# Start of a hybrid decoder step on one core: first loads and casts reordered, the norm's broadcast moved behind the second pair

## The chip, the cores and the metric

The kernel runs on one core of a Trainium2 chip. The metric is the device time of one launch in microseconds (us); lower is better. A core has TensorE (PE: matrix products), VectorE (DVE), ScalarE (ACT), GpSimd (POOL) and SyncE (SP, which here only issues loads and stores); all run beside each other and wait for each other through semaphores.

## What is computed

One step of a decoder block on T = 520 columns (512 prompt tokens and 8 sampled ones): a half-step SwiGLU FFN, a mixer with attention and state-space heads, a second half-step FFN, and a last norm. The change lies in the two FFNs, whose reference is:

```python
def rmsnorm(x, g):
    xf = x.astype(F32)
    y = xf * lax.rsqrt(jnp.mean(xf * xf, axis=-1, keepdims=True) + EPS) * g.astype(F32)
    return y.astype(x.dtype)

def half_ffn(x, norm_g, w_in, w_out):
    h = rmsnorm(x, norm_g)
    gate, up = jnp.split(h @ w_in, 2, axis=-1)
    return x + FFN_RESIDUAL * ((jax.nn.silu(gate) * up) @ w_out)
```

`D_MODEL` is 1024 and `D_FF` 2816, so `w_in` has 22 gate and 22 up tiles of 128 columns.

## The kernel before

**Layout.** x is held transposed, as 8 tiles `x[k]` of 128 x 520 (k runs over the 1024 rows of the model width). Each f32 value is kept as a rounded high part and a remainder: `cut` (lines 352 to 356) makes `qh` on ScalarE (line 354) and `ql` on VectorE (line 355) out of a weight tile of 128 x 512; `split_x` (lines 227 to 234) does the same for x times the norm's gain, giving `hh` (line 232) and `hl` (line 233). `mm3` (lines 212 to 224) then makes three matmuls for each product: high by high, high by remainder, remainder by high. A row of 520 columns is done in two halves f of 260, each in a bank of PSUM of its own.

**One FFN** is `ffn_comb` (lines 403 to 476); it is called twice, here named pass 1 (before the mixer) and pass 2 (after it). Its first loop runs over pairs j = 0 to 4 of a gate tile and an up tile. Pair 0 is done k by k for gate and up at once, pairs 1 to 4 first the gate (8 k's, 48 matmuls) and then the up. Pairs 0, 1 and 2 multiply x that is not yet normalised; their results are multiplied by the norm r afterwards. From pair 3 on, x itself has been normalised.

**The norm.** In pass 1 `first_squares` (lines 247 to 255) squares the eight tiles on ScalarE and adds them up in `acc` on VectorE. `rsq1` (lines 257 to 272) sums `acc` over the partitions on TensorE (line 263), takes the inverse root (line 265, a power on GpSimd, lines 283 to 286) and writes it to a diagonal `dg` (lines 269 and 271). `rsq_half2` (lines 496 to 505) spreads `dg` over all partitions with three matmuls (line 502) into the spare columns of the banks of pair 0, and ScalarE copies the result to `r` (line 504). `gate_up2` (lines 507 to 525) multiplies the banks of a pair by r (lines 516 and 517), which sets these banks free, and makes the hidden tile. `normalize` and `two` (lines 527 to 540) normalise x (line 531) and split it (`ch`, line 537, and `cl`, line 539).

**Banks.** PSUM has eight banks of this pool and a pair takes four. So pair 2 takes the banks of pair 0, and pair 3 those of pair 1.

**Order.** In `run`, the beginning stands under `manual_schedule` for SP, ScalarE and VectorE: these follow the order in which the code is written. In `ffn_comb` TensorE follows the written order, and the scheduler of the tile framework places the instructions of the other engines, among them the casts of later weight tiles, which may so come to stand in the middle of the manual part. Each load is counted on one of eight counters in turn (`DMAHW0` to `DMAHW7` in the lists below, SP and ScalarE together), and a load waits until the load before it on its counter has landed. Raw weights have names `fr` for pair 0 (`fr00`: gate, first half of the k's, `fr10`: up, `fr01`, `fr11`: second halves) and `br2`, `br3`, `br4` ... for the tiles after it: `br2` is the gate of pair 1, `br3` its up, `br4` the gate of pair 2. `setup_cache` loads five small tables (`pt`, `ci`, `v16`, `scv` on ScalarE's queue) and computes indices `ix` and `cwh` from them on VectorE.

Of the kernel before, what the change touches and what calls it, by code (L numbers as in the profile page):

```python
# [10 lines left out]
ALU = mybir.AluOpType  # L11
# [3 lines left out]
T = 520  # L15
NP = 512
HF = 260
D = 1024
# [126 lines left out]
class Program:  # L145
# [81 lines left out]
    def split_x(self, k, gcol):  # L227
        nc = self.nc
        hi = self.t2(f"hh{gcol}_{k}", F32R)
        lo = self.t2(f"hl{gcol}_{k}", F32R)  # L230
        g = self.vec[:, gcol + k:gcol + k + 1]
        nc.scalar.activation(hi[:, :T], self.x[k][:, :T], AF.Copy, scale=g)
        nc.vector.scalar_tensor_tensor(lo[:, :T], self.x[k][:, :T], g, hi[:, :T], ALU.mult, ALU.subtract)  # L233
        self.h[k] = (hi, lo)

# [167 lines left out]
    def ffn_comb(self, gcol, source, after=None, early=None):  # L403

        nc = self.nc
        self.b_more()
        with self.tc.manual_schedule(engines={mybir.EngineType.PE}):
            hid, held, r, norm = [], None, None, None
            for j in range(SFROM):
# [12 lines left out]
                for gu in range(len(pair), 2):  # L422
                    w = self.b_take()
                    ps = [self.bank1("gu") for _ in range(2)]
                    for k in range(8):
                        for f in range(2):
                            self.mm3(ps[f][:, :HF], w, k, self.h[k], f * HF, k == 0, k == 7)
                    pair.append(ps)
                    if held is not None:
                        r = self.rsq_half2(norm, held)  # L430
                        hid.append(self.gate_up2(*held, r))
                        held = None
                        h = self.normalize(r, gcol)
                    self.b_more()
                if r is None:
                    norm, held = self.rsq1(self.acc, D, pair[1][0][:, HF:], True), pair
                else:
                    hid.append(self.gate_up2(*pair, r if j < SRAW else None))
# [103 lines left out]
    def combos(self):  # L542
# [22 lines left out]
        for i, t in enumerate(tt):  # L565
            nc.vector.scalar_tensor_tensor(t[:, b], t[:, a], -1.0, self.xn[i + 4][:, a], ALU.mult, ALU.subtract)
# [157 lines left out]
    def setup_cache(self):  # L724
# [6 lines left out]
        for c0, c1, mul, col in ((0, 128, 128, 0), (128, 160, 32, 1), (160, 168, 8, 2)):  # L731
            nc.vector.tensor_scalar(ix[:, c0:c1], pt[:, c0:c1], mul, None, ALU.mult)
            nc.vector.tensor_tensor(ix[:, c0:c1], ix[:, c0:c1], ci[:, col:col + 1].to_broadcast([128, c1 - c0]), ALU.add)
# [7 lines left out]
        nc.vector.tensor_scalar_mul(self.cwh, self.vec[:, V_CW:V_CW + 40], 0.5)  # L741
# [781 lines left out]
    def run(self):  # L1523
        nc, tc, a = self.nc, self.tc, self.a
        with (
# [22 lines left out]
            with tc.manual_schedule(engines={mybir.EngineType.SP, mybir.EngineType.Activation, mybir.EngineType.DVE}):  # L1548
                warm = pc.tile([128, 1], F32, name="warm")
                nc.scalar.dma_start(self.vec, a["vec"])  # L1550
                nc.scalar.dma_start(self.x[0][:, :T], a["xT"][0])
# [3 lines left out]
                for c in range(2):  # L1555
                    for n in range(2):
                        nc.sync.dma_start(first[n][c], self.bu[n][1][:, c * 512:c * 512 + 512])
                    for k in range(4 if c else 1, 8 if c else 4):
                        nc.sync.dma_start(self.x[k][:, :T], a["xT"][k])
                self.b_load()  # L1560
                nc.sync.dma_start(self.cf, a["cf"])
                self.b_w = {n: ([], []) for n in range(2)}
                for k in range(8):
                    if k in (0, 4):
                        for n in range(2):
                            for q, t in zip(self.b_w[n], self.cut(first[n][k // 4])):
                                q.append(t)
                    self.split_x(k, V_F1)
                self.b_load()
                nc.sync.dma_start(self.cb, a["cb"])  # L1570
                self.b_load()
                self.first_squares()
                self.b_split()
# [48 lines left out]
```

## Time and profile before

| what | value |
| --- | --- |
| time, median of 3 runs | 1107.99 us (1107.32 to 1109.2) |
| the profiled execution's own time | 1109.26 us |
| its span, first to last instruction | 1107.5 us |
| PE busy | 1073.4 us, 97% |
| DVE, ACT, POOL busy | 719.4, 501.4, 264.6 us |
| PE on the chain that ended last | 86% |
| loads and stores | 204.30 MB, mean 184 GB/s |

TensorE is busy nearly all the time, so what counts is when it stands still, and at which clock it runs. The rows below show idle times with what ended them, and the granted clock behind some of them.

### The profile page before, as it was taken

To read this page: it belongs to the slowest core of one execution; us is meant where nothing else is said; L and a number is where in the kernel's file an instruction comes from. 1 tells how busy PE (TensorE), PEld (TensorE's weight loads), DVE (VectorE), ACT (ScalarE), POOL (GpSimd) and SP (SyncE) were. 2 spreads that over 40 slices of the span, in tenths; PEclk is the share of its full clock that TensorE was granted. 3 is DMA by queue.
4 is the path that set the end of the run, shared out by engine and by line. 5 is a ranking of instruction groups with operands and counts; after the bars stand their busy time and mean duration, and the time that the engine had idled before them with its cause. 6 is when DMAs were issued, how large, how long until landed. Compare 5 with 4: busy or idle time off the path is not lost.

```text
span 1107.5 us, 23255 instructions
## 1 busy us (share of the span) xinstructions
PE 1073.4 (97%) x9079; PEld 991.7 (90%) x9079; DVE 719.4 (65%) x1499; ACT 501.4 (45%) x1077; POOL 264.6 (24%) x261
## 2 busy tenths in 40 slices
PE   8999999999999999999999998999999999999995
PEld 6999999999999988776756676999999999999995
DVE  6985477467555679363768868449855764685563
ACT  6452355256244422456622555245534543562452
POOL 0001001110105667575343321120020011101013
PEclk9999999999999999999999999999999999999997
DMA  8539358455616788688899735163484584556302
GB/s 272 136 104 255 92 144 222 107 139 170 161 47 205 269 305 298 232 281 305 292 379 406 268 131 197 47 221 99 133 226 104 131 232 98 147 176 150 109 11 78
DMA packets 93917, 204.30 MB, mean 184 GB/s; under 512 B 13384, under 2 KB 21960, under 8 KB 89712
## 3 DMA queue, kind: packets, MB, share of 16 engines
q1 hardware_dynamic: 68736, 124.19, 34.4%
q0 software_dynamic: 22336, 77.08, 24.6%
q10 hardware_dynamic: 2736, 1.56, 0.5%
q8 instruction: 71, 1.16, 0.4%
q14 instruction: 38, 0.31, 0.1%
HBM read 191.78 MB, written 11.01 MB: 183 GB/s over the span
## 4 chain that ended last, share of the span: by engine, by line
PE 86%; DVE 5%; DMA 3%; issue 2%; ACT 2%; POOL 1%; ACTq 0%; DVEq 0%; SPq 0%; POOLq 0%
PE fo L223 7%; PE fo L224 7%; PE fo L222 7%; PE cx L578 6%; PE cx L577 6%; PE cx L576 6%; PE mps L222 4%; PE mps L223 3%; PE mps L224 3%; PE gu L222 3%; PE gu L224 3%; PE gu L223 3%; PE cy L576 3%; PE cy L577 3%; PE cy L578 3%; PE sps L1060 2%
## 5 line engine op out<-in xcount | busy, mean ns | idle before, releaser
L354 ACT CAST qh<-br 128x512 fp32r<-128x512 f32 (+1 forms) x310 | 168.2, 585 | 120.0 <-PE fo L223 57.5
L355 DVE TENSOR_TENSOR ql<-br,qh 128x512 fp32r<-128x512 f32 (+1 forms) x310 | 188.8, 644 | 44.1 <-ACT qh L354 19.3
L223 PE MATMUL fo<-hidl,qh 128*128 128x260 f32 x640 | 181.3, 283 | 0.8 <-DVE hidl L613 0.8
L222 PE MATMUL fo<-hidh,qh 128*128 128x260 f32 x640 | 181.1, 283 | 0.0
L224 PE MATMUL fo<-hidh,ql 128*128 128x260 f32 x640 | 180.8, 283 | 0.0
L578 PE MATMUL cx<-ch,ql 128*128 128x260 f32 x544 | 153.8, 283 | 0.0
L577 PE MATMUL cx<-cl,qh 128*128 128x260 f32 x544 | 153.6, 282 | 0.0
L576 PE MATMUL cx<-ch,qh 128*128 128x260 f32 x544 | 153.5, 282 | 0.0
L223 PEld LDWEIGHTS fo<-hidl,qh 128*128 128x128 f32 x640 | 120.4, 188 | 1.6 <-DVE hidl L613 1.5
L222 PEld LDWEIGHTS fo<-hidh,qh 128*128 128x128 f32 x640 | 120.5, 188 | 0.0
L224 PEld LDWEIGHTS fo<-hidh,ql 128*128 128x128 f32 x640 | 120.5, 188 | 0.0
L222 PE MATMUL mps<-hh,whi 128*128 128x260 f32 x384 | 113.3, 295 | 2.3 <-DVE raw L880 2.3
L348 POOL DMA_DIRECT2D br<-in_wi x34 | 29.7, 874 | 354.7 <-DMA br<-in_wi 204.7
L223 PE MATMUL mps<-hl,whi 128*128 128x260 f32 x384 | 109.7, 286 | 0.6 <-DVE hl L233 0.6
L224 PE MATMUL mps<-hh,wlo 128*128 128x260 f32 x384 | 109.4, 285 | 0.0
L576 PEld LDWEIGHTS cx<-ch,qh 128*128 128x128 f32 x544 | 102.4, 188 | 0.0
L578 PEld LDWEIGHTS cx<-ch,ql 128*128 128x128 f32 x544 | 102.4, 188 | 0.0
L577 PEld LDWEIGHTS cx<-cl,qh 128*128 128x128 f32 x544 | 102.3, 188 | 0.0
L786 POOL DMA_INDIRECT kv<-in_kc,ix x66 | 74.0, 1122 | 59.5 <-PE cy L578 25.7
L222 PEld LDWEIGHTS mps<-hh,whi 128*128 128x128 f32 x384 | 73.3, 191 | 13.5 <-issue 10.4
L577 PE MATMUL cy<-cl,qh 128*128 128x260 f32 x272 | 77.0, 283 | 0.0
L576 PE MATMUL cy<-ch,qh 128*128 128x260 f32 x272 | 76.9, 283 | 0.0
(430 smaller groups left out, 2705.4 us busy)
## 6 DMA issues: line engine op xcount, KB each, us to landing
br<-in_wi SPq DMA_DIRECT2D x206, 256.0 KB, 3.9
br<-in_wi POOLq DMA_DIRECT2D x68, 256.0 KB, 4.7
br<-in_wo SPq DMA_DIRECT2D x56, 256.0 KB, 2.9
wraw<-in_wm SPq DMA_DIRECT2D x24, 512.0 KB, 6.3
br<-in_wo SPq DMA_DIRECT2D x48, 128.0 KB, 2.7
kv<-in_kc SPq DMA_DIRECT2D x22, 256.0 KB, 4.6
spill<-xr SPq DMA_DIRECT2D x16, 260.0 KB, 3.3
xr<-spill SPq DMA_DIRECT2D x16, 260.0 KB, 5.5
```

The source lines that it names most:

```text
L222: mm(out, lhsT=hi[:, ks], rhs=xh[:, cs], start=start, stop=False)
L223: mm(out, lhsT=hi[:, ks], rhs=xl[:, cs], start=False, stop=False)
L224: mm(out, lhsT=lo[:, ks], rhs=xh[:, cs], start=False, stop=stop)
L348: nc.gpsimd.dma_start(s1, u[:, h[1]], accum_op=ALU.add)
L354: self.nc.scalar.copy(hi[:, :n], raw[:, :n])
L355: self.nc.vector.tensor_sub(lo[:, :n], raw[:, :n], hi[:, :n])
L576: mm(out, lhsT=hi[:, ks], rhs=xh, start=start and i == 0, stop=False, skip_group_check=True)
L577: mm(out, lhsT=hi[:, ks], rhs=xl, start=False, stop=False, skip_group_check=True)
L578: mm(out, lhsT=lo[:, ks], rhs=xh, start=False, stop=i == 3, skip_group_check=True)
L786: nc.gpsimd.indirect_dma_start(out=pages[j], out_offset=None, in_=a["kc"], in_offset=bass.IndirectOffsetOnAxis(ap=self.ix[:, 4 * n + j:4 * ...
L1060: nc.tensor.matmul(self.sbank[32 * hp:32 * hp + 32, cs], lhsT=self.qz[:, c0:c0 + 32], rhs=rhs(hp), start=(n % 16 == 0), stop=(n % 16 == 15 ...
```

## The change

It does four things. The first loads are all issued by SP in the order in which TensorE uses them, x[0] first, and the casts of the first weights are interleaved with the splits of x. The loads of pair 1 and of the gate of pair 2 are asked for right behind the split of x[3] (`issue_after`), and the cast of pair 1's gate is placed ahead of `first_squares`. The index computations of `setup_cache` are placed behind `self.mark`, the last of the combinations that are built for pair 5 on. And in `ffn_comb`, in both passes, the sum over the partitions (`rsq1`) moves from the end of pair 0 to before k = 6 of pair 1's gate, while the broadcast, the multiplications of pair 0 and `normalize` move from the end of pair 1's gate to the end of its up. The calls, tiles and matmuls stay the same in number.

```diff
--- before.py
+++ after.py
@@ -230,8 +230,8 @@
         lo = self.t2(f"hl{gcol}_{k}", F32R)
         g = self.vec[:, gcol + k:gcol + k + 1]
         nc.scalar.activation(hi[:, :T], self.x[k][:, :T], AF.Copy, scale=g)
-        nc.vector.scalar_tensor_tensor(lo[:, :T], self.x[k][:, :T], g, hi[:, :T], ALU.mult, ALU.subtract)
         self.h[k] = (hi, lo)
+        return nc.vector.scalar_tensor_tensor(lo[:, :T], self.x[k][:, :T], g, hi[:, :T], ALU.mult, ALU.subtract).ins
 
     def square_x(self, k, adder=None):
         nc = self.nc
@@ -423,17 +423,18 @@
                     w = self.b_take()
                     ps = [self.bank1("gu") for _ in range(2)]
                     for k in range(8):
+                        if j == 1 and k == 6 and gu == 0:
+                            norm = self.rsq1(self.acc, D, held[1][0][:, HF:], True)
                         for f in range(2):
                             self.mm3(ps[f][:, :HF], w, k, self.h[k], f * HF, k == 0, k == 7)
                     pair.append(ps)
-                    if held is not None:
+                    if j == 1 and gu == 1:
                         r = self.rsq_half2(norm, held)
                         hid.append(self.gate_up2(*held, r))
-                        held = None
                         h = self.normalize(r, gcol)
                     self.b_more()
                 if r is None:
-                    norm, held = self.rsq1(self.acc, D, pair[1][0][:, HF:], True), pair
+                    held = pair
                 else:
                     hid.append(self.gate_up2(*pair, r if j < SRAW else None))
                 if j == SRAW - 1:
@@ -563,7 +564,8 @@
             x0, x1 = self.xn[i], self.xn[i + 4]
             nc.vector.scalar_tensor_tensor(t[:, a], ss[i][:, b], -1.0, x0[:, a], ALU.mult, ALU.subtract)
         for i, t in enumerate(tt):
-            nc.vector.scalar_tensor_tensor(t[:, b], t[:, a], -1.0, self.xn[i + 4][:, a], ALU.mult, ALU.subtract)
+            self.mark = nc.vector.scalar_tensor_tensor(
+                t[:, b], t[:, a], -1.0, self.xn[i + 4][:, a], ALU.mult, ALU.subtract).ins
         halves(self.two(*tt), 6, 4)
 
     def product(self, out, w, p, start):
@@ -728,9 +730,10 @@
         nc.scalar.dma_start(pt, a["pt"])
         nc.scalar.dma_start(ci, a["ci"])
         ix = pc.tile([128, 168], I32, name="ix")
-        for c0, c1, mul, col in ((0, 128, 128, 0), (128, 160, 32, 1), (160, 168, 8, 2)):
-            nc.vector.tensor_scalar(ix[:, c0:c1], pt[:, c0:c1], mul, None, ALU.mult)
-            nc.vector.tensor_tensor(ix[:, c0:c1], ix[:, c0:c1], ci[:, col:col + 1].to_broadcast([128, c1 - c0]), ALU.add)
+        with self.tc.issue_after(self.mark):
+            for c0, c1, mul, col in ((0, 128, 128, 0), (128, 160, 32, 1), (160, 168, 8, 2)):
+                nc.vector.tensor_scalar(ix[:, c0:c1], pt[:, c0:c1], mul, None, ALU.mult)
+                nc.vector.tensor_tensor(ix[:, c0:c1], ix[:, c0:c1], ci[:, col:col + 1].to_broadcast([128, c1 - c0]), ALU.add)
         self.ix, self.ptr = ix, pt
         v16 = pc.tile([16, 3], F32, name="v16")
         nc.scalar.dma_start(v16, a["v16"])
@@ -738,7 +741,8 @@
         self.scv = pc.tile([128, 8, 4, 8], F32, name="scv")
         nc.scalar.dma_start(self.scv[:, :, 0:3, :], a["sc"].rearrange("p (c j b) -> p c j b", j=3, b=8))
         self.cwh = pc.tile([128, 40], F32, name="cwh")
-        nc.vector.tensor_scalar_mul(self.cwh, self.vec[:, V_CW:V_CW + 40], 0.5)
+        with self.tc.issue_after(self.mark):
+            nc.vector.tensor_scalar_mul(self.cwh, self.vec[:, V_CW:V_CW + 40], 0.5)
         self.kv_t, self.kv_pool = {}, {}
         self.ring = [n for n in range(64) if n not in KEARLY]
         self.sm = {}
@@ -1548,29 +1552,37 @@
             with tc.manual_schedule(engines={mybir.EngineType.SP, mybir.EngineType.Activation, mybir.EngineType.DVE}):
                 warm = pc.tile([128, 1], F32, name="warm")
                 nc.scalar.dma_start(self.vec, a["vec"])
-                nc.scalar.dma_start(self.x[0][:, :T], a["xT"][0])
+                nc.sync.dma_start(self.x[0][:, :T], a["xT"][0])
                 nc.scalar.activation(warm, self.mhalf, AF.Silu)
                 first = [[self.r2t(f"fr{n}{c}") for c in range(2)] for n in range(2)]
                 self.b_loaded = self.b_cut = 2
-                for c in range(2):
-                    for n in range(2):
-                        nc.sync.dma_start(first[n][c], self.bu[n][1][:, c * 512:c * 512 + 512])
-                    for k in range(4 if c else 1, 8 if c else 4):
-                        nc.sync.dma_start(self.x[k][:, :T], a["xT"][k])
-                self.b_load()
-                nc.sync.dma_start(self.cf, a["cf"])
+                def fetch(n, c):
+                    nc.sync.dma_start(first[n][c], self.bu[n][1][:, c * 512:c * 512 + 512])
+
+                fetch(0, 0)
+                for k in range(1, 8):
+                    if k in (1, 5):
+                        fetch(1, k // 4)
+                    if k == 4:
+                        fetch(0, 1)
+                    nc.sync.dma_start(self.x[k][:, :T], a["xT"][k])
                 self.b_w = {n: ([], []) for n in range(2)}
                 for k in range(8):
-                    if k in (0, 4):
-                        for n in range(2):
+                    for n in range(2):
+                        if k in (0, 4):
                             for q, t in zip(self.b_w[n], self.cut(first[n][k // 4])):
                                 q.append(t)
-                    self.split_x(k, V_F1)
-                self.b_load()
-                nc.sync.dma_start(self.cb, a["cb"])
-                self.b_load()
+                        if n == 0:
+                            mark = self.split_x(k, V_F1)
+                    if k == 3:
+                        with tc.issue_after(mark):
+                            self.b_load()
+                            nc.sync.dma_start(self.cf, a["cf"])
+                            self.b_load()
+                            nc.sync.dma_start(self.cb, a["cb"])
+                            self.b_load()
+                self.b_split()
                 self.first_squares()
-                self.b_split()
 
             def early():
                 self.leave("pg")
```

**ScalarE, start of pass 1**, from the split of x[5] on. Before:

```order
L232 ACTIVATE hh0_5_170<-x5_86,vec_76 128x520 [waits DMAHW6_49]
L232 ACTIVATE hh0_6_174<-x6_87,vec_76 128x520 [waits DMAHW7_49]
L354 CAST qh_328<-br3_182 128x512 [waits DMAHW4_49]
L232 ACTIVATE hh0_7_178<-x7_88,vec_76 128x520 [waits DMAHW0_49]
L252 ACTIVATE acc_191<-x0_81 128x520
```

Now:

```order
L232 ACTIVATE hh0_5_179<-x5_86,vec_76 128x520 [waits DMAHW6_49]
L354 CAST qh_328<-br3_158 128x512 [waits DMAHW4_49]
L232 ACTIVATE hh0_6_183<-x6_87,vec_76 128x520 [waits DMAHW7_49]
L232 ACTIVATE hh0_7_187<-x7_88,vec_76 128x520 [waits DMAHW0_49]
L354 CAST qh_191<-br2_153 128x512 [waits DMAHW1_49]
L354 CAST qh_195<-br2_155 128x512 [waits DMAHW2_49]
L252 ACTIVATE acc_199<-x0_81 128x520
```

The cast of the first half of `br3` stood behind the split of x[6] and now stands ahead of it; the casts of `br2` now come before the squares. The loads that these casts wait for stand now on SP like this, where counter 1 was last used by the load of `scv` on ScalarE's queue:

```order
L1568 DMA x6_87<-in_xT 128x520 [waits DMAHW7_49]
L1568 DMA x7_88<-in_xT 128x520 [waits DMAHW0_49]
L340 DMA br2_153<-in_wi1 128x512 [waits DMAHW1_49]
L340 DMA br2_155<-in_wi1 128x512 [waits DMAHW2_49]
L1580 DMA cf_77<-in_cf 128x530 [waits DMAHW3_49]
L340 DMA br3_158<-in_wi1 128x512 [waits DMAHW4_49]
```

**VectorE, pass 1**, from the last addition to `acc` to line 265. Before:

```order
L254 TENSOR_TENSOR acc_191<-acc_191,sq_211 128x520 [waits DVE_49,Activation_49]
L355 TENSOR_TENSOR ql_215<-br2_129,qh_214 128x512 [waits DMAHW1_49,Activation_49]
L355 TENSOR_TENSOR ql_219<-br2_131,qh_218 128x512 [waits DMAHW2_49,Activation_49]
L355 TENSOR_TENSOR ql_329<-br3_182,qh_328 128x512 [waits DMAHW4_49]
L265 TENSOR_SCALAR rsqt_340<-gu_230 128x5 [waits PE_49]
```

Now:

```order
L355 TENSOR_TENSOR ql_333<-br3_160,qh_332 128x512 [waits DMAHW5_49,Activation_49]
L254 TENSOR_TENSOR acc_199<-acc_199,sq_219 128x520 [waits DVE_49]
L355 TENSOR_TENSOR ql_409<-br4_163,qh_408 128x512 [waits DMAHW7_49,Activation_49]
L355 TENSOR_TENSOR ql_413<-br4_165,qh_412 128x512 [waits DMAHW0_49,Activation_49]
L355 TENSOR_TENSOR ql_530<-br5_336,qh_529 128x512 [waits DMAHW1_49,PE_49,Activation_49]
L355 TENSOR_TENSOR ql_534<-br5_338,qh_533 128x512 [waits DMAHW2_49,PE_49,Activation_49]
L355 TENSOR_TENSOR ql_604<-br6_416,qh_603 128x512 [waits DMAHW3_49,PE_49,Activation_49]
L355 TENSOR_TENSOR ql_608<-br6_418,qh_607 128x512 [waits DMAHW4_49,PE_49,Activation_49]
L265 TENSOR_SCALAR rsqt_378<-gu_230 128x5 [waits PE_49]
```

Between `acc` and line 265 three remainders of weights stood, and now there are six.

**TensorE, pass 1, end of pair 1.** The broadcast is followed by pair 1's up before, and now by pair 2's gate. Before:

```order
L502 MATMUL gu_229<-dg_352,cf_77 128x252 [waits DVE_49]
L502 MATMUL gu_231<-dg_352,cf_77 128x16 [waits DVE_49]
L222 MATMUL gu_479<-hh0_0_142,qh_328 128x260
```

Now:

```order
L503 MATMUL gu_229<-dg_390,cf_77 128x252 [waits DVE_49]
L503 MATMUL gu_231<-dg_390,cf_77 128x16 [waits DVE_49]
L222 MATMUL gu_553<-hh0_0_133,qh_408 128x260 [waits DVE_49]
```

What the new first matmul waits for on VectorE is the multiplication that sets the first bank of pair 0 free (line 517 of the changed kernel). The same holds in pass 2.

## Rows read from the trace of the kernel before

**Rows 1.** Windows, both stretches up to pair 3; columns: us, busy by engine, PEclk, DMA.

```profile
0.00:24.13 24.13, 18.74 (x108) 14.64 (x109) 14.37 (x29) 16.44 (x28) 0.19 (x4) 0.93 0.86 288
742.70:768.00 25.30, 25.30 (x211) 25.21 (x210) 21.70 (x46) 12.68 (x24) 3.07 (x3) 1.00 0.51 146
```

**Rows 2.** What PE waited for, first 35 us: us in total, times, longest.

```profile
PE gu L223 <- DVE hl L233: 2.1, 1, 2.1
...
PE gu L263 <- DVE acc L254: 0.7, 1, 0.7
```

**Rows 3.** Window with the granted TensorE clock (PEclk), start of pair 0.

```profile
10.38:13.36 2.98, 2.98 (x13) 2.98 (x14) 2.98 (x5) 2.37 (x4) 0.00 (x0) 0.50 1.04 367
```

**Rows 4.** Timeline of ACT and its queue, start: start us, us, what, idle before.

```profile
5.52 0.62 ACT L354 CAST qh<-fr 128x512 fp32r<-128x512 f32 x1 [0.57 <-DMA fr<-in_wi]
5.52 0.33 ACTq L729 DMA_DIRECT2D ci<-in_ci  x1
...
6.38 0.62 ACTq L739 DMA_DIRECT2D scv<-in_sc  x1
...
16.21 0.62 ACT L354 CAST qh<-br 128x512 fp32r<-128x512 f32 x1 [2.69 <-DMA br<-in_wi]
```

**Rows 5.** Timeline of SP's queue, the load of `br3` (both halves).

```profile
12.22 0.80 SPq L340 DMA_DIRECT2D br<-in_wi  x2
```

**Rows 6.** Weights `br` in the first 20 us: issue to landing.

```profile
DMA to landing us min/median/max: 4.0/5.6/5.7
```

**Rows 7.** Timeline of DVE, start to pair 1's first multiplication.

```profile
8.49 0.39 DVE L732 TENSOR_SCALAR ix<-pt 128x128 int32<-128x128 int32 x3 [1.63 <-DMA pt<-in_pt]
9.19 0.47 DVE L733 CUSTOM_DVE_ANT_0 ix<-ci,ix 128x256 uint16<-128x256 uint16 x3 [0.30 <-DMA ci<-in_ci]
...
13.46 2.09 DVE L233 SCALAR_TENSOR_TENSOR hl<-x,vec,hh 128x520 fp32r<-128x520 f32 x3
17.50 0.76 DVE L233 SCALAR_TENSOR_TENSOR hl<-x,vec,hh 128x520 fp32r<-128x520 f32 x1 [1.95 <-ACT hh L232]
18.55 5.52 DVE L254 TENSOR_TENSOR acc<-acc,sq 128x520 f32<-128x520 f32 x7 [0.29 <-ACT sq L252]
...
25.80 0.16 DVE L265 TENSOR_SCALAR rsqt<-gu 128x5 f32<-128x5 f32 x1
...
31.24 2.49 DVE L355 TENSOR_TENSOR ql<-br,qh 128x512 fp32r<-128x512 f32 x4
33.65 0.42 DVE L516 TENSOR_TENSOR gt<-gu,r 128x260 f32<-128x260 f32 x1
...
47.07 0.42 DVE L516 TENSOR_TENSOR gt<-gu,r 128x260 f32<-128x260 f32 x1
```

**Rows 8.** Timeline of PE, the first matmul of pair 3 in pass 1.

```profile
49.52 0.28 PE L222 MATMUL gu<-ch,qh 128*128 128x260 f32 x1
```

**Rows 9.** Timeline of PE in pass 2: broadcast, pair 1's up, pair 3.

```profile
749.60 1.14 PE L502 MATMUL gu<-dg,cf 128*128 128x252 f32 x6
750.60 0.37 PE L222 MATMUL gu<-hh,qh 128*128 128x260 f32 x1
...
767.95 0.28 PE L222 MATMUL gu<-ch,qh 128*128 128x260 f32 x1
```

**Rows 10.** Timeline of DVE in pass 2: first multiplications of pairs 0 and 1.

```profile
751.06 0.43 DVE L516 TENSOR_TENSOR gt<-gu,r 128x260 f32<-128x260 f32 x1
...
765.09 0.42 DVE L516 TENSOR_TENSOR gt<-gu,r 128x260 f32<-128x260 f32 x1
```

**Rows 11.** Timeline of PE in the mixer: two waits, in brackets.

```profile
439.49 0.36 PE L222 MATMUL mps<-hh,whi 128*128 128x260 f32 x1 [2.34 <-DVE raw L880]
...
577.56 1.10 PE L1251 MATMUL stp<-xdd,bn 128*128 128x256 f32 x4 [1.92 <-DVE xdd L1248]
```

**Rows 12.** Windows right behind these two waits.

```profile
439.40:443.00 3.60, 3.51 (x18) 3.54 (x19) 2.52 (x5) 1.01 (x3) 2.88 (x3) 0.60 0.77 209
577.50:582.00 4.50, 4.44 (x28) 2.17 (x28) 4.20 (x9) 0.59 (x1) 0.94 (x1) 1.00 1.00 390
```

## The prediction, before the changed kernel was run

> **What bounds the kernel now.** I read the busy times first, then the windows of the two stretches that the change touches, then what TensorE waited for in them, and last the timelines of the engines that it waited for. What to see: pass 1 has something to win and pass 2 has nothing. Up to 24.13 us TensorE is busy for 18.74 us and the clock is 0.93; in pass 2, from `rsq1` to pair 3, it is busy for 25.30 of 25.30 us at full clock [rows 1]. In pass 1 it waits 2.1 us for the remainder of x[0] and later 0.7 us for `acc` [rows 2], and behind the first wait it runs 2.98 us at the lower of its two levels, 1.2 instead of 2.4 GHz [rows 3]. One matmul of 260 columns costs 0.1205 us at the full clock: from 750.60 to 767.95 there are 48 of pair 1's up and 96 of pair 2 [rows 9], and 17.35 / 144 = 0.1205.
>
> **The start.** x[0] is loaded first and its split no longer stands behind the index computations, for whose tables VectorE waited until 8.49 and 9.19 [rows 7]. The second big load landed at 5.5 [rows 4]; `fr00` is second now, so ScalarE casts it at 5.5, splits x[0] at 6.1, VectorE makes the remainder from 6.8 to 7.55, and TensorE starts in earnest at 7.6. Without further waits it would need x[6] after 72 matmuls, at 7.6 + 8.7 = 16.3.
>
> The index computations now stand behind the last combination. What queues behind them is needed for pair 5, which is 192 matmuls or 23 us behind the start of pair 3; so they cost nothing here, and 0.9 us (0.39 + 0.47) if that cover were gone. SP's reads of the page table move too, to places where SP waits for a counter anyhow: nothing.
>
> **A new wait at x[6].** ScalarE is in order, and the cast of `br3` now stands ahead of the split of x[6]. When does `br3` land? `br2`, the first of the late loads, waits for counter 1, that is for `scv`. `scv` goes out once `fr00` has landed, at 5.55. Before, the load that waited for `scv` went out at 12.22, 5.84 us after `scv` at 6.38 [rows 4, 5]. So `br2` goes out at 11.4, not when x[3] is split; three issues of 0.4 us [rows 5] later, at 12.6, `br3`. It took 4.0 us before, issued at 12.22 and cast at 16.21 [rows 4, 5], so it lands at 16.6. The bounds: a load of `scv` as short as that of `ci`, 3.7 us (issued 5.52, used at 9.19 [rows 4, 7]), gives 14.45; a load of `br3` of 5.7 us, the longest [rows 6], gives 18.25. I take 16.6, since these are the same tiles in much the same queue. From that cast to the start of VectorE's split behind the next one were 1.29 us (16.21 to 17.50 [rows 4, 7]): x[6]'s remainder starts at 17.9.
>
> The Trainium skill, page "DMA: Bandwidth & Descriptors", section "Anatomy of one DMA — SWDGE (gpsimd) path", gives 2.0 us plus the bytes at 436 GB/s for one transfer on another issuing path. An estimate by that page puts `scv` at 2.2 and `br3` at 2.6 us, the cast at 11.6, and the end where rival C below has it. The trace disagrees, with 5.84 and 4.0 us.
>
> **VectorE from there to pair 3.** It has no gap of its own, so this is a sum [rows 7]: the remainders of x[6] and x[7] 2 x 0.67 (three take 2.09); three remainders of weights at 0.60 (31.24 to 33.65 is four), 1.8; six additions to `acc`, 5 x 0.80 + 0.6 (seven take 5.52, each waiting for the one before), 4.6; a remainder 0.6, the last addition 0.6; six remainders 3.6; from line 265 to the end of `dg` 5.44 before (25.80 to 31.24), less the one remainder that is no longer in between, 4.9; two remainders 1.2. Together 18.7, so pair 0 is multiplied from 36.6. TensorE agrees: `acc` is ready 9.0 us after 17.9, at 26.9; the sums take 1.0, then 12 + 48 matmuls 7.2, so the broadcast starts at 35.2; and in pass 2 the multiplication came 1.46 us behind the broadcast (749.60 to 751.06 [rows 9, 10]): 36.7. I take 36.7.
>
> Two new waits follow, because the banks are now set free late. Pair 2's gate needs the first bank of pair 0, free 0.42 us after 36.7, at 37.1. Pair 3 needs the first bank of pair 1, which VectorE reaches behind eight normalisations and eight remainders of x: 13.42 us after pair 0's first multiplication (33.65 to 47.07 [rows 7]), by the same 23 instructions as before, and 0.42 for itself: 50.55. TensorE would be there at 37.1 + 96 x 0.1205 = 48.7 and waits 1.85. Before, pair 3 started at 49.52 [rows 8]. **Pass 1: +1.0 us**, all that the early start won being given back; its bounds, from the landing of `br3`, are -1.1 and +2.7.
>
> **Pass 2** has only the losses. Count from the broadcast. Before, the next matmul came 1.0 us later (749.60 to 750.60 [rows 9]). Now it waits for the bank until 1.46 + 0.42 = 1.9: +0.9. Pair 3 can start at 1.9 + 11.57 = 13.45 by TensorE, but the bank of pair 1 is free at 1.46 + 14.03 (751.06 to 765.09 [rows 10], the same 24 instructions) + 0.42 = 15.9: +2.45. **Together +3.35 us.** Before, both lay beside pair 1's up, whose 48 matmuls are 5.8 us. The bounds are narrow, 0.3 us, since each length has its row.
>
> **The clock.** A wait of 2.34 us for VectorE was followed by a window at 0.60 mean granted clock, one of 1.92 us by a window at 1.00 [rows 11, 12]. The wait before pair 3 is 1.85 in pass 1 and 2.45 in pass 2, so I let the clock fall in pass 2 alone. The price: 0.40 x 3.60 = 1.4 us in that window; at the start 2.98 us at 0.50 are 1.5 [rows 12, 3]. **+1.5 us**, with 0 and 1.7 as its bounds. The Trainium skill, page "TensorE: Matmul & The Clock Gate", section "Loop structure matters more than you think", says that VectorE copying a result out of PSUM does not break TensorE's warmth. By that rule this term is nothing and the sum is rival B's. The row at 439.49 speaks against it, a wait for VectorE with a slow window behind it.
>
> **The sum**: 1.0 + 3.35 + 1.5 = +5.85 us. The profiled execution took 1109.26 us, its span 1107.5 and 1.76 around it; that is 1.27 over the median of 1107.99. So I expect 1115.1 for that one, and 1113.8 as the median. Behind pair 3 the order is nearly as before and TensorE works without a pause, so I carry the difference to the end.
>
> **Rivals.**
> - B: the clock holds. For it: 2.45 is hardly more than 2.34, and TensorE was busy throughout before it. Against: those two rows. +4.35, 1112.3.
> - C, not slower: the cast of `br3` costs nothing and the early start is kept. Place: ScalarE, ahead of x[6]; price: 1 us at pair 3 for each us that `br3` lands earlier, until TensorE itself is the bound: 7.6 + (96 + 36 + 60 + 96) x 0.1205 + 1.0 + 1.9 + the 1.85 is 47.05, 2.5 us earlier than before. With the clock holding, the total is +0.85, 1108.8. It decides from a landing at 14.4 on, where the total is 2.2. Against it: my lower bound is 14.45, and it needs the clock too. For it: a chain of estimated landings.
> - D: the clock falls in pass 1 also, behind the 1.85 us or the wait at x[6]. For it: 1.85 is close to 1.92, which has one row alone. +7.35, 1115.3.
>
> **Numbers.** The forecast 0.45, B 0.28, D 0.12, C 0.10, something else 0.05. A measurement of this kernel can tell about 0.2%, 2.2 us, from no change. Forecast, B and D are slower by more; C is within it; to be faster both passes would have to lose less than I can construct. That gives slower 0.85, same 0.12, faster 0.03. The range: at its low end the clock holds and pass 1 is at its lower bound, -1.1 + 3.35 = +2.25, 1110.2; at its high end 2.7 + 3.35 + 1.7 + 1.5 = +9.25, 1117.2. It leaves out C, and I round to 1110 and 1117.
>
> **What would show it.** In the new profile: TensorE in earnest at about 7.6; a ScalarE wait for `br` ahead of x[6], until about 16.6; pair 3 of pass 1 near 50.5 with a wait for line 517 of the changed kernel; in pass 2 two waits for the same line, 0.9 and 2.45 us; a lower granted clock behind the second. I am wrong if the two waits of pass 2 are missing (then the banks did not bind), or if ScalarE does not wait for `br3` (then pass 1 wins).

## The result: slower, by about the forecast amount, with two of its terms wrong in size

The changed kernel takes 1114.26 us (median, 1113.19 to 1116.67) against 1107.99. The medians lie 6.3 us apart; the recorded ratio is 1.0065, interval 1.0047 to 1.0083, which is +7.2 us with 5.2 to 9.2. Timed again later (`e11_changed_again`) the ratio was 1.0054 (1.0034 to 1.0074), and the medians lay 6.9 us apart. The gains and losses below go by the recorded ratios. The forecast was 1113.8 and a range of 1110 to 1117.

The page of the changed kernel, busy times and the chain that ended last; TensorE's share of the chain was 86% before and is 81% now, VectorE's was 5% and is 8%:

```profile
span 1114.0 us, 23258 instructions
...
PE 1076.7 (97%) x9079; PEld 993.6 (89%) x9079; DVE 720.1 (65%) x1499; ACT 501.4 (45%) x1077; POOL 263.9 (24%) x261
...
PE 81%; DVE 8%; DMA 4%; ACT 3%; issue 3%; POOL 1%; SPq 0%; DVEq 0%; ACTq 0%; POOLq 0%
```

What TensorE waited for in the changed kernel (us in total, times, longest), first from 0 to 60 us, the stretch of [rows 2], then from 735 to 800:

```profile
PE gu L222 <- ACT hh L232: 3.6, 2, 2.7
PE gu L222 <- DVE gt L517: 2.4, 2, 1.7
...
PE gu L223 <- DVE hl L234: 0.6, 2, 0.4
```

```profile
PE gu L222 <- DVE gt L517: 3.1, 2, 2.3
```

The 2.1 us for the first remainder and the 0.7 for `acc` are gone. In their place stand 2.7 us for the split of x[6], and in each pass two waits for line 517, the multiplication that sets a bank free. In pass 2 TensorE had not waited at all [rows 1].

Windows of the changed kernel: up to the end of the wait at x[6], behind it, around pair 3 of pass 1, and behind the wait before pair 3 of pass 2 (PEclk is the third number from the end):

```profile
0.00:18.87 18.87, 13.93 (x84) 10.38 (x84) 7.26 (x12) 8.96 (x14) 0.19 (x4) 1.00 0.88 279
18.87:25.70 6.83, 6.32 (x27) 6.02 (x28) 6.13 (x10) 6.83 (x14) 0.00 (x0) 0.50 0.97 359
51.80:56.00 4.20, 2.54 (x22) 2.54 (x22) 4.20 (x9) 1.04 (x2) 0.00 (x0) 1.00 0.01 4
...
773.20:776.63 3.43, 3.43 (x19) 3.43 (x18) 3.34 (x8) 1.27 (x2) 0.00 (x0) 0.50 0.00 0
```

The clock fell behind the wait at x[6] and behind the one in pass 2, and not behind the 1.66 us in between.

To see where the time went, each execution is cut at three matmuls, whose starts stand in TensorE's timelines (pair 3 of pass 1, the first of pass 2, pair 3 of pass 2), and at its end. The first column is a time, the other three are distances. The last four rows come from a slower chip, on which more below.

| kernel | pair 3, pass 1 | to the first of pass 2 | to its pair 3 | to the end |
| --- | --- | --- | --- | --- |
| before [rows 8, 9] | 49.52 | 681.73 | 36.70 | 339.55 |
| before, second profile (`e10`) | 49.61 | 679.11 | 36.70 | 339.63 |
| changed | 53.49 | 679.06 | 40.17 | 341.24 |
| changed, second profile (`e11`) | 50.91 | 681.82 | 40.17 | 341.20 |
| `e1` new start alone | 56.07 | 682.53 | 36.80 | 339.67 |
| `e2` norm's new place alone | 52.77 | 678.54 | 40.16 | 341.71 |
| `e3` br3 behind | 49.28 | 679.21 | 40.16 | 340.94 |
| `e4` pair 1 first | 50.30 | 679.74 | 37.83 | 340.41 |
| `e9` spread | 44.59 | 677.58 | 36.76 | 339.86 |
| `e5` before, slower chip | 49.66 | 724.56 | 36.70 | 339.50 |
| `e6` scv on another queue | 51.22 | 720.95 | 40.17 | 342.45 |
| `e7` squares first, old norm | 47.95 | 726.58 | 36.70 | 339.64 |
| `e8` squares first, new norm | 51.49 | 723.76 | 40.18 | 341.02 |

In the third column the norm's late place shows alike to 0.1 us wherever it stands as the change has it. Pass 1 is not alike: the two profiles of the changed kernel differ by 2.6 us. And the second column moves by 2.7 us between two profiles of one kernel, in either direction. It holds the rest of pass 1 as well; that rest, up to the last matmul of the pass's output product (`fo`), takes 323.6 to 324.1 us in all nine profiles that are not from the slower chip, so the movement is the mixer's, and the moved index computations cost no more than half a microsecond there. They were not tried alone.

### The profile page after: what moved, and what is told of

Read it like the earlier page. It is cut to its first block, busy times and chain, and to the rows that moved or that the text cites. A ratio compares the mean times of both kernels' runs of the same rounds, so it can differ in the third digit from the quotient of the medians.

```text
span 1114.0 us, 23258 instructions
## 1 busy us (share of the span) xinstructions
PE 1076.7 (97%) x9079; PEld 993.6 (89%) x9079; DVE 720.1 (65%) x1499; ACT 501.4 (45%) x1077; POOL 263.9 (24%) x261
## 4 chain that ended last, share of the span: by engine, by line
PE 81%; DVE 8%; DMA 4%; ACT 3%; issue 3%; POOL 1%; SPq 0%; DVEq 0%; ACTq 0%; POOLq 0%
PE fo L223 7%; PE fo L224 7%; PE fo L222 7%; PE cx L578 6%; PE cx L579 6%; PE cx L580 6%; PE mps L222 3%; PE mps L223 3%; PE mps L224 3%; PE cy L578 3%; PE cy L579 3%; PE cy L580 3%; PE sps L1064 3%; PE gu L222 2%; PE gu L223 2%
## 5 line engine op out<-in xcount | busy, mean ns | idle before, releaser
L222 PEld LDWEIGHTS mps<-hh,whi 128*128 128x128 f32 x384 | 72.4, 188 | 13.3 <-issue 10.2
```

The source lines that it names most:

```text
L222: mm(out, lhsT=hi[:, ks], rhs=xh[:, cs], start=start, stop=False)
```

## The experiments

### The two halves of the change, each alone

`e1_start_only` is the changed kernel with the loop over pairs put back:

```diff
-                        if j == 1 and k == 6 and gu == 0:
-                            norm = self.rsq1(self.acc, D, held[1][0][:, HF:], True)
...
-                    if j == 1 and gu == 1:
+                    if held is not None:
                         r = self.rsq_half2(norm, held)
                         hid.append(self.gate_up2(*held, r))
+                        held = None
                         h = self.normalize(r, gcol)
...
-                    held = pair
+                    norm, held = self.rsq1(self.acc, D, pair[1][0][:, HF:], True), pair
```

> Only the start's reordering is kept, the norm stands where it stood before. Theory M (the late cast of br3 stops the start, and the norm's late place stops both passes): the wait at x[6] stays (2.7 us, then half clock to about 25.7); acc is ready at 28.2 as in the changed kernel, and now TensorE stands about 3 us for it; pair 3 of pass 1 starts 25.4 us behind the first sum, at 53.6, +4.1 against before; pass 2 is as before, no wait for pair 0's or pair 1's banks, no fall of the clock. Total +1.3 to +4.1 (the mixer gave back 2.8 us in the changed kernel's profile), 1109.3 to 1112.1. Rival N (the norm's late place is the whole loss, the new start only wins): pair 3 at 47 to 48.5, total -1 to -2.5, 1105.5 to 1107.

Measured: ratio 1.0069 (1.005 to 1.0087), +7.6 us. What TensorE waited for up to 60 us, and a window that begins inside the longest wait:

```profile
PE gu L263 <- DVE acc L254: 5.3, 1, 5.3
PE gu L222 <- ACT hh L232: 3.0, 2, 2.0
```

```profile
24.67:34.91 10.24, 7.72 (x36) 7.72 (x37) 7.29 (x20) 3.57 (x8) 2.60 (x2) 0.50 0.41 122
```

Rival N falls: the new start costs as much by itself as the whole change. Theory M had the place right and the size wrong, pair 3 standing at 56.07 instead of 53.6: the wait for `acc` was 5.3 us instead of 3, since the clock held behind x[6] this time and TensorE was there at 21.9, while `acc` was ready at 27.13, only 1.1 us sooner than in the changed kernel. The clock was at half for 10.24 us, of which TensorE worked 7.72. Pass 2 is as before.

`e2_norm_only` is the reverse of this edit, made in the kernel before.

> Only the norm is moved, the start is the one of before. Theory M: the 0.7 us for acc goes; in pass 1 TensorE waits 0.9 us before pair 2 and 1.9 before pair 3, which starts at 51.3, +1.8; in pass 2 the same two waits, 0.8 and 2.3 us, +3.5, and behind the second the clock falls for 3.4 us, +1.5. Total +6.8, less up to 2.8 in the mixer: 1112.0 to 1114.8. Rival S (the start's order is the whole loss, the norm's place costs nothing): 1108, no wait for the multiplication by r ahead of pair 3.

Measured: 1.0065 (1.004 to 1.009), +7.2 us. In pass 2:

```profile
PE gu L222 <- DVE gt L517: 3.1, 2, 2.3
```

The same line as in the changed kernel. Rival S falls. Pass 1 lost 3.2 us instead of 1.8: the clock was at half from 7.6 to 14.4, and TensorE waited 0.7 us for a remainder. Each half costs about 7 us and both together cost 7, so the parts overlap in pass 1: with the new start `acc` comes late, and the later `rsq1` does not wait for it, which saves the 5.3 us of `e1`.

### br3 behind, and pair 1 first

`e3_br3_behind`, a second `b_split` in the written order, so that the scheduler can't place the casts of `br3` ahead of x[6]:

```diff
                 self.b_split()
+                self.b_split()
                 self.first_squares()
```

> The changed kernel with the casts of br3 behind those of br2, so behind the splits of x[6] and x[7]. Theory M: no wait at x[6], no half clock at the start; TensorE reaches the sums earlier, and pair 3 of pass 1 starts at about 48.1 instead of 53.5, where VectorE's chain lets it; pass 2 keeps its +3.5 and the clock's +1.5. Total -5.4 against the changed kernel, 1108.9; 1111.7 if what the mixer gave back there goes with it. Rival L (the loads of the second pair land too late for any order: TensorE stands for br2 or acc instead): pair 3 at 52 or later, 1113 to 1114.

Measured: 1.0049 (1.0033 to 1.0066), +5.4 us, pair 3 at 49.28. The wait at x[6] is gone and the clock holds to the end of pass 1, as theory M has it, but the gain is smaller. Up to 60 us:

```profile
PE gu L222 <- DVE gt L517: 2.5, 2, 1.7
PE gu L263 <- DVE acc L254: 2.1, 1, 2.1
```

The wait moved on to `acc`: ScalarE now waits for `br2` and `br3` ahead of the squares. Against the mean of the two profiles of the changed kernel (52.2) pass 1 won 2.9 us; I had counted from the later of the two. So rival L is half right: TensorE does stand for `acc`, and the median of 1113.06 us lies where L has it; pair 3, which L has at 52 or later, lies near theory M's 48.1.

`e4_pair1_first` multiplies pair 1 by r before x is normalised, and leaves it out where it stood:

```diff
                         r = self.rsq_half2(norm, held)
                         hid.append(self.gate_up2(*held, r))
+                        hid.append(self.gate_up2(*pair, r))
                         h = self.normalize(r, gcol)
...
-                else:
+                elif j > 1:
                     hid.append(self.gate_up2(*pair, r if j < SRAW else None))
```

> The changed kernel with pair 1 multiplied by r before x is normalised, in both passes, so that pair 1's banks come free early. Theory M: the wait before pair 3 of pass 2 goes from 2.3 to about 0.5 us (now for the first split tile), and with it the fall of the clock behind it: -1.8 - 1.5; in pass 1 from 1.66 to about 0.3. Total -4.6 against the changed kernel, 1109.6. Rival K (the clock's fall in pass 2 has another cause than this wait): the slow stretch at 773 stays, 1111.1. Rival V (VectorE is the bound whatever its order: pair 3 waits as long for its split tiles): 1114.

Measured: 1.0008 (0.9995 to 1.0022), +0.9 us, 5 to 6 less than the changed kernel. TensorE's waits from 735 to 800, and the window around pair 3 of pass 2:

```profile
PE gu L222 <- DVE gt L518: 0.8, 1, 0.8
PE gu L223 <- DVE cl L541: 0.6, 1, 0.6
```

```profile
766.00:775.00 9.00, 8.36 (x69) 8.15 (x69) 9.00 (x18) 4.42 (x9) 0.00 (x0) 1.00 0.11 29
```

The bank's 2.3 us are 0.6 for a split tile, and the clock stays at 1.00. From the first matmul of pass 2 to the end it is 378.24 us against 381.41, 3.2 less, where 3.3 were expected. In pass 1 the wait of 1.66 us is gone too. Rivals K and V fall: the order on VectorE was the bound, not its work, and the slow stretch comes with that wait. `e4` is one profile, but the other six without that wait have no such stretch either, and all six with it do.

### scv on another queue

Four runs (`e5` to `e8`) fell on a chip where the kernel before takes 1155.24 us; they are compared with each other. `e5_before_again` is the kernel before, unchanged.

> The kernel before, unchanged, profiled a second time. Theory M holds that the 2.8 us which the changed kernel seems to win in the mixer are the chance of one execution: the mixer of before shows other waits and other slow stretches of the clock this time, and from pair 3 of pass 1 to the broadcast of pass 2 it is 1 us or more shorter than in the first profile, while pair 3 of pass 1 stands at 49.5 within 1 us and pass 2 loses nothing. Rival P (the changed kernels really win in the mixer, because they come to it with another timing): the mixer is as long as in the first profile, within 0.5 us.

What differs there lies between about 350 and 565 us, in the end of pass 1 and in the mixer. TensorE stands idle for nothing that the profile shows, 19.4 us in all, and from pair 3 to pass 2 the granted clock is at half for 41.0 us, where it was 6.8 in the first profile of before. Two of the waits in `e5` (`fo` is the end of pass 1), and a window of it (PEclk third from the end):

```profile
PE sps L1060 <- issue: 6.2, 13, 1.0
...
PE fo L222 <- issue: 3.5, 6, 1.3
```

```profile
330.00:470.00 140.00, 120.86 (x953) 105.49 (x953) 79.72 (x152) 37.66 (x67) 69.04 (x65) 0.88 0.65 214
```

In the first profile of before the clock of the same window was 0.99. So `e5` says nothing on the mixer of the first chip, and cannot tell theory M from rival P; pair 3 (49.66) and pass 2 (36.70) are as there.

`e6_scv_other_queue`:

```diff
-        nc.scalar.dma_start(self.scv[:, :, 0:3, :], a["sc"].rearrange("p (c j b) -> p c j b", j=3, b=8))
+        nc.gpsimd.dma_start(self.scv[:, :, 0:3, :], a["sc"].rearrange("p (c j b) -> p c j b", j=3, b=8))
```

> The changed kernel with the load of scv on GpSimd's queue, so that no load of SP waits for it. Theory M (br2 went out at 11.14 because its counter waited for scv): br2 goes out at about 9.2, right behind the last x; br3 at about 11.6 (its counter then waits for x[4]) instead of 12.47, and is cast at 16.4 to 17.0 instead of 17.87; the wait at x[6] shrinks from 2.7 to 1.3 to 1.9 us. Rival Q (the queue or the memory is the limit, not the counter): br3 is cast at 17.5 or later and the wait stays at 2.4 or more.

The issues of the weights on SP's queue, and the cast of `br3`, in `e6`:

```profile
9.19 0.90 SPq L340 DMA_DIRECT2D br<-in_wi  x2
...
10.62 0.93 SPq L340 DMA_DIRECT2D br<-in_wi  x2
```

```profile
16.93 0.62 ACT L354 CAST qh<-br 128x512 fp32r<-128x512 f32 x1 [4.29 <-DMA br<-in_wi]
```

`br2` goes out at 9.19 as expected, so the counter and `scv` did hold it, and rival Q's times are not met. `br3` goes out at 10.62, a microsecond sooner than expected, and takes 6.3 us. The wait at x[6] was 1.4 us, inside theory M's span; but in `e11`, with `scv` where it was, the cast came at 16.32, and the changed kernel did not run on the chip of `e6`. What the counter is worth at x[6] is therefore not settled: how long the weights take to land moves as much.

### Squares ahead of the casts, with either place of the norm

`e7` puts the squares first and the norm where it stood; `e8` has the same start and the norm of the changed kernel.

```diff
-                self.b_split()
                 self.first_squares()
+                self.b_split()
+                self.b_split()
```

> The new start with the squares ahead of the casts of br2 and br3, and the norm where it stood before. Theory M: no wait at x[6], acc ready at about 18.6, the sums at 18.8 instead of 24.13 and pair 3 of pass 1 18.35 us behind a broadcast at 25.6 to 26.5, at 44.3 to 45.5, -4 to -5.2 against before; pass 2 as before. Total 1103 to 1104.5. Rival L (the second pair's loads are the limit of pass 1): TensorE waits for br2 or br3 instead, pair 3 at 47 or later, 1106 or more.

> As the run beside it, but with the norm's late place of the changed kernel. Theory M: the broadcast of pass 1 at 31.4, pair 3 15.3 us behind it, at 46.7, -2.8 against before, and pass 2 loses 3.5 and 1.5 for the clock: total +2.2, 1110.2; against the run beside it the norm's place costs 7 us, though nothing waits for acc in either. Rival N2 (the norm's late place costs only where something else is late too): within 2 us of the run beside it.

Measured: `e7` 0.9985 (0.9969 to 1.0001), pair 3 at 47.95; `e8` 1.0043 (1.0028 to 1.0058), pair 3 at 51.49. Between them 0.58%, 6.7 us (the medians: 6.2), where 7 were expected, and rival N2 falls: the late place costs this also with an early `acc`. Of it 4.9 are in pass 2 (40.18 + 341.02 against 36.70 + 339.64). But both miss their own times, and pair 3 of `e7` stands where rival L has it, at 47 or later. TensorE's waits up to 60 us in `e7`, then in `e8`:

```profile
PE gu L263 <- DVE acc L254: 2.1, 1, 2.1
```

```profile
PE gu L222 <- DVE gt L517: 2.4, 2, 1.6
PE gu L224 <- DVE ql L355: 2.0, 1, 2.0
```

In `e7` `acc` was ready at 21.0 instead of 18.6. ScalarE's seven squares end at 18.6, one every 0.54 us, but VectorE's seven additions follow each other at 0.79 us:

```profile
15.46 5.53 DVE L254 TENSOR_TENSOR acc<-acc,sq 128x520 f32<-128x520 f32 x7 [0.29 <-ACT sq L252]
```

The clock fell for 3.41 us behind the wait. In `e8` TensorE waited for the remainders of `br2`, which stood behind those additions, and the clock fell for 3.41 us there too. ScalarE casts `br2` and `br3` without a wait for a load in both. So VectorE's additions and their order are the limit, and not the loads, as rival L has it.

### A version that beats both

`e9_spread` takes from each what had shown a use: the new start; `br2` cast in the middle of the squares, `br3` behind them; in pass 1 alone the sums and the broadcast late, but each spread into the matmuls that hide it; pair 1 multiplied ahead of `normalize`; pass 2 as in the kernel before.

```diff
         for k in range(8):
+            if k == 4:
+                self.b_split()
             sq = self.t2("sq") if k else acc
...
-                        if j == 1 and k == 6 and gu == 0:
+                        if first and j == 1 and (gu, k) == (0, 4):
                             norm = self.rsq1(self.acc, D, held[1][0][:, HF:], True)
+                        if first and j == 1 and (gu, k) == (1, 6):
+                            r = self.rsq_half2(norm, held)
+                            hid.append(self.gate_up2(*held, r))
...
                     hid.append(self.gate_up2(*pair, r if j < SRAW else None))
+                    if first and j == 1:
+                        h = self.normalize(r, gcol)
...
-                self.b_split()
                 self.first_squares()
+                self.b_split()
```

(`first` is true in pass 1; in pass 2 the old lines stand.)

> The new start; the casts of br2 in the middle of the squares and those of br3 behind them; in pass 1 the sums before k = 4 of pair 1's gate, the broadcast before k = 6 of its up, and pair 1 multiplied by r before x is normalised; pass 2 as in the kernel before. Theory M: no wait of TensorE over 1.7 us up to pair 3, so no half clock there; acc ready at about 22.2, the sums there, the broadcast at 30.4, pair 2 at 32.9, pair 3 at 44.4 to 45.2, -4.4 to -5.1 against the 49.5 of before; pass 2 unchanged. Total -3.5 to -5 against before. Rival L (in pass 1 the loads or VectorE's work as a whole are the bound, and any order ends near 48): -1.5 or less.

Measured: 0.9954 (0.9936 to 0.9972), 5.1 us faster than before (3.1 to 7.1), a little more than the expected 3.5 to 5; its median of 1103.11 us is 11.6 below that of the changed kernel beside it. TensorE's waits up to 60 us, and the window from its start in earnest to pair 3:

```profile
PE gu L222 <- ACT hh L232: 1.2, 1, 1.2
PE gu L223 <- DVE hl L234: 0.4, 1, 0.4
PE gu L265 <- DVE acc L256: 0.2, 1, 0.2
```

```profile
7.27:44.59 37.32, 37.09 (x303) 36.79 (x304) 34.31 (x66) 26.68 (x50) 3.48 (x3) 1.00 0.80 252
```

From 7.27 on TensorE is busy for 37.09 of 37.32 us at full clock, and pair 3 starts at 44.59, inside the expected 44.4 to 45.2. Rival L falls. What each of its four moves is worth was not tried apart. The expectation took half clock to come only behind waits over 1.7 us, which does not hold: `e11` has it behind 1.62.

### Both kernels profiled again

> The kernel before, unchanged, profiled once more. Theory M (part of what the changed kernel seems to win in the mixer is the chance of one execution): other waits and slow stretches of the clock in the mixer than in the first profile, and its length off by 1 us or more, if the chip is as quick as the first. Rival P: the same length within 0.5 us. Pair 3 of pass 1 at 49.5 within 1 us and no loss in pass 2 in any case.

> The changed kernel, unchanged, timed beside the two others on one chip. Theory M: pass 1 loses 3 to 4 us (the fall of the clock behind the wait at x[6] included) and pass 2 3.5 and 1.5; the whole is slower by 5 to 9 us, and the mixer's part differs from that of the first profile. Rival P: the mixer gives back 2.8 us as in the first profile, within 0.5 us.

What TensorE waited for from 400 to 720 us, in the first profile of before and then in `e10`:

```profile
PE attps L1035 <- ACT pT L1023: 3.1, 2, 2.4
...
PE ops L1167 <- DMA kv<-in_vc,ix: 1.6, 1, 1.6
```

```profile
PE attps L1035 <- ACT pT L1023: 1.1, 2, 0.7
...
PE ops L1167 <- DMA kv<-in_vc,ix: 0.5, 1, 0.5
```

The mixer of before is 2.6 us shorter in its second profile, and that of the changed kernel 2.8 longer. Rival P falls: what the changed kernel seemed to win there is chance. Much of it is the clock: in the mixer it is at half for 6.8 and then 3.4 us in the two profiles of before, and for 3.4 and then 10.2 us in those of the changed kernel, in which TensorE's idle times there differ by 0.7 us only. In pass 1, `e11` against the first profile of the change: the cast of `br3`, and pair 3:

```profile
16.32 0.62 ACT L354 CAST qh<-br 128x512 fp32r<-128x512 f32 x1 [3.68 <-DMA br<-in_wi]
```

```profile
50.91 0.36 PE L222 MATMUL gu<-ch,qh 128*128 128x260 f32 x1 [1.67 <-DVE gt L517]
```

With `br3` there at 16.32, TensorE waited 1.6 us at x[6] instead of 2.7, the clock fell for 3.41 us instead of 6.83, and pair 3 is at 50.91. So pass 1 lost 1.4 us, less than the 3 to 4 that were expected.

## Why the prediction held, step by step

**The start: right.** 7.6 was forecast, 7.63 measured, 7.21 in `e11`.

**br2 behind scv: right.** The chain that ended last, in the changed kernel (start, length, what):

```profile
5.38 5.75 DMA scv<-in_sc
11.14 0.33 SPq L340
...
12.47 5.38 DMA br<-in_wi
17.87 0.62 ACT qh L354
```

`scv` goes out at 5.38 and `br2` 5.76 us behind it, where 5.84 were taken.

**The landing of br3: undersized.** The step "it took 4.0 us before" chose the shortest of [rows 6]; it took 5.4 us, and 5.2 in `e11`. So the cast came at 17.87 instead of 16.6; in `e11`, where the load of `scv` was shorter, at 16.32. The upper bound of 18.25 held. The estimate that the prediction worked out from the Trainium skill, page "DMA: Bandwidth & Descriptors", section "Anatomy of one DMA — SWDGE (gpsimd) path", for another issuing path, was 2.6 us; the trace disagrees twofold.

**VectorE to pair 3: right in length, wrong in what binds.** From the cast of `br3` to the complete `acc` are 10.37 us (forecast 10.3), from the broadcast to pair 2 1.93 (1.9) and from there to pair 3 13.51 (13.45). But the broadcast itself, at 38.05 instead of 35.2, was not held by VectorE: `acc` was complete at 28.24, and TensorE came to the sums only at 29.71.

```profile
27.55 0.69 DVE L254 TENSOR_TENSOR acc<-acc,sq 128x520 f32<-128x520 f32 x1
29.71 1.17 PE L263 MATMUL gu<-cf,acc 128*128 128x1 f32 x10
```

**The clock in pass 1: the step that failed.** "So I let the clock fall in pass 2 alone" ordered the waits of [rows 11] by their length and looked only at the two before pair 3. The fall came behind the wait at x[6], 6.83 us of it in one profile and 3.41 in the other. That is rival D, for its second reason. Pass 1 cost 4.0 us in the first profile and 1.4 in the second, against +1.0 forecast and 2.7 as its upper bound. In the first, 1.3 of the 3.0 us over the forecast are the later cast of `br3` and 1.5 the slow TensorE that came to the sums behind `acc`; in the second the cast was early and TensorE came 0.5 behind `acc` (27.14 against 26.68). That the fall was the cause of this lateness is worked out: TensorE was busy for 6.32 us at half clock and would have needed 3.2 less at full clock, so it would have been there before `acc`.

**Pass 2: right.** +3.47 us in both profiles, 3.35 forecast; the two waits are 0.80 and 2.33, 0.9 and 2.45 forecast. All six profiles with the late norm as the change has it show it alike, and `e1`, `e7` and `e9`, which have it early in pass 2, at most 0.1 us.

**The clock in pass 2: right in its size, with a reason that does not hold.** From pair 3 to the end 341.2 us against 339.6, +1.6 for a forecast of 1.5; over the six profiles it is 340.94 to 342.45. Behind the wait of 2.3 us the granted clock was 0.50 in all six, and 1.00 in `e4`, where that wait was gone. But the reason, that 2.34 us of waiting in the mixer cost the clock and 1.92 did not [rows 11, 12], is one execution's chance. The same two waits, first of the changed kernel and then of `e11`, each with a window behind it:

```profile
443.86 0.36 PE L222 MATMUL mps<-hh,whi 128*128 128x260 f32 x1 [2.30 <-DVE raw L884]
443.86:447.46 3.60, 3.60 (x44) 3.46 (x48) 2.52 (x5) 1.01 (x3) 2.96 (x3) 1.00 0.76 232
```

```profile
577.17 1.10 PE L1255 MATMUL stp<-xdd,bn 128*128 128x256 f32 x4 [1.91 <-DVE xdd L1252]
578.38:581.80 3.42, 3.42 (x12) 1.41 (x5) 1.99 (x4) 0.51 (x1) 0.94 (x1) 0.50 1.00 401
```

Here the longer wait left the clock at full and the shorter one was followed by half. So that the clock fell in pass 2 as forecast is in part luck. The Trainium skill, page "TensorE: Matmul & The Clock Gate", section "Loop structure matters more than you think", says that VectorE copying a result out of PSUM does not break the warmth, of a loop whose next matmuls follow immediately. Here they had to wait for the bank, and the clock fell.

**The sum.** With the first profile alone, 4.0 + 3.5 + 1.7 = 9.2 us, of which the mixer hid 2.7 by chance; with the second 1.4 + 3.5 + 1.6 = 6.5. The recorded ratios give 7.2 and 6.0, the medians 6.3 and 6.9. So the forecast of 5.85 was near for pass 2's sake, and low in pass 1 by 0.4 to 3.0. That the span of the first profile grew by only 6.5 us, near the forecast, is luck: the mixer's chance made up for most of what pass 1 lost beyond it.

## What to carry to other kernels

Before a hand-over of banks is moved later, find the next user of each bank and count the instructions that stand ahead of the multiplication on its engine: here 23 instructions, eight normalisations and eight remainders among them, kept pair 1's multiplications back by 13.4 us and became TensorE's wait, and putting these multiplications ahead of them took back 3.2 of the 5.2 us that pass 2 had lost. A stall that is removed from the front of a chain moves to its next link, so an early start is worth only what the slowest chain behind it, here ScalarE's squares and VectorE's sum, lets through. And two profiles of one kernel should be cut at the same landmarks before a difference outside the change is explained.

## What was not expected of the hardware

The length of a wait alone did not decide the clock. It fell behind the 1.6 us at x[6] in `e11`, not behind the 1.6 to 1.7 us before pair 3 of pass 1 in six profiles, and not behind 2.0 us at x[6] in `e1` (the window 18.00:24.67 there is at 1.00). A wait of 2.1 us for `acc` was followed by half clock in `e7` and not in `e3`. In the mixer, in the nine profiles that are not from the slower chip, the wait of 2.2 to 2.3 us for `raw` was followed by half clock in four (before, `e10`, `e1`, `e11`) and the wait of 1.9 us for `xdd` in four (`e1`, `e3`, `e4`, `e11`), and by full clock in the other five each time. In the changed kernel, `e1` and `e2` the clock also fell between 461 and 465 us with no wait over 0.15 us in the 9 us before. How long it stayed at half differed too: 3.4 us behind 2.9 at x[6] in `e4`, 6.8 behind 2.7 in the changed kernel, and 10.2 from inside the longest wait, 5.3 us, in `e1`. What sets these apart is left open.

The slow clock at the start of the kernel before costs next to nothing: in `e10` it lasted 6.8 us instead of 3.4, and pair 3 came at 49.61 instead of 49.52, as `acc` was the later of the two; TensorE's wait for it shrank from 0.7 to 0.3 us instead. In `e2`, where nothing waits for `acc`, the 6.8 us were among the causes of a later pair 3.
